# A list scheduler that counts changes between array tiles as TensorE time

## Chip, cores and metric

The kernel runs on one core of one Trainium2 chip. The metric is the device time of one execution in microseconds, from the first to the last instruction and what lies around them; lower is better. Times before and after are compared by the median of several runs.

## What is computed

A network of four layers on 512 positions with 1024 features, in fp32. The first block has a state-space layer and a latent-attention layer, each followed by a gated feed-forward layer; the second block has two layers that run three kinds of attention side by side. Cut to what matters:

```python
x = x + s5_mixer(rms_norm(x, mix_norm[0]), ...)            # layer 0: a state-space scan over 512 positions
x = x + swiglu_ffn(rms_norm(x, ffn_norm[0]), ...)
k, v = mla_shared_kv(rms_norm(x, kv_in_norm), ...)         # layer 1: latent attention, 16 heads
o = causal_block_attention(mla_queries(...), k, v)
x = x + o @ mla_w_o
x = x + swiglu_ffn(rms_norm(x, ffn_norm[1]), ...)
h = _layernorm(x, ...)                                      # second block
for layer in range(2):
    proj = h @ w_in[layer]                                  # three kinds of attention share it
    ya = _differential_attention(...) * silu(ag)            # 4 heads of 128, two softmaxes each
    yb = _forgetting_attention(...) * silu(bg)              # 4 heads of 64
    yc = _stick_breaking_attention(...) * silu(cg)          # 4 heads of 64
    h = _layernorm(ALPHA * h + concat(ya, yb, yc) @ w_out[layer], ...)
```

## The kernel before

Activations lie feature by feature: eight tiles of 128 features by 512 positions. A large product is made from three full-array products per 128x128 piece of the weights, since weights and activations are each split into a high and a low part of the fp32r type (`mm3`, line 651; names `wh_r`, `wl_r` for weights, `xh_r`, `xl_r` for activations). Weights come by DMA, ScalarE makes the high part, VectorE the low part.

Three stages use narrower tiles of TensorE's 128x128 array, named by rows*columns of the tile:

- The state-space scan (`s5_k`, `s5_x`, `s5_y`, `s5_o`, lines 995 to 1111): fp32 products on 128*32, 128*64 and 64*64 tiles. An fp32 product is two passes, two records in the trace.
- Latent attention (`attend`, line 1610): per head pair and block of 128 queries, two score products, softmax on VectorE and ScalarE, transposes of the probabilities (`nc.tensor.transpose`, one pass each, full array) and products with the values. Two heads share a PSUM bank; the values product of one head writes columns 0 to 63 of the array, that of the other columns 64 to 127 (`tile_position=(0, 64 * e)`). 32 such units; later `kv_part` and `q_part` products are mixed in.
- The second block's attentions (`attend_c`, `attend_a`, `attend_b`, `values`, from line 1777): the same shape of work, 32 units a layer; `values` (line 1897) is the one with 64-column tiles, the differential attention's product with the values uses the full array.

The order of all instructions is not written by hand. `Plan` (line 76) records every operation with its dependencies, then `schedule` (line 287) makes an order for all engines: twelve rounds of a forward list scheduling (`forward`, line 312) and a backward pass (line 370) that sets due times for the next round. The round with the earliest end by the planner's own costs is emitted. On TensorE, `forward` takes from the ready products the one with the earliest due time, plus a penalty where a weight load is longer than the product before it hides:

```python
i = min((i for i in ready[e] if at[i] <= t + 1e-9),
        key=lambda i: (due[i] + self.SWITCH * max(0.0, ops[i][6] - before), i))
t, before = max(t, free[e] + ops[i][6] - before), ops[i][1]
```

`ops[i][6]` is the load time of the product's weights, `before` the duration of the product ahead. The planner knows nothing of array tiles here. Where it foresees a gap on TensorE of more than 0.37 us and a PSUM bank is free, it puts idle-fill products (`fillers`, line 270, `ident` times `ident`) into it, so that the engine's clock stays up. Every recorded operation is issued from one helper, so the trace names L263 for nearly all; idle-fill products have L276. After the change the two lines are L265 and L278.

Of the kernel before, what the change touches and what calls it, by code (L numbers as in the profile page):

```python
# [20 lines left out]
P = 128  # L21
# [54 lines left out]
class Plan:  # L76
# [6 lines left out]
    SWITCH = 30.0  # L83
    TICK, DUTY = 10.24 / 3, 0.3735
    FILL, FLOOR = 0.22, 0.95
    parted = None
    EVERY_TABLE = (AF.Copy, AF.Identity, AF.Square)

# [25 lines left out]
    def switch(self, close, open):  # L114

        deps = {i: 0.0 for g in close for i in self.groups[g].used}
        for g in close:
            for i in self.groups[g].gate:
                deps[i] = 0.0
        i = len(self.ops)  # L120
        gone = [self.groups[g] for g in close]
        new = [Group(self, g) for g in open]

        def fn():
            for g in gone:
                g.exit()
            for g in new:
                g.enter(self.tc)

        self.ops.append((self.NONE, 0.0, 0.0, deps, self.clock, fn, 0.0, 0.0, None))  # L130
        for g in new:
            g.gate = [i]
            self.groups[g.name] = g
        return [Rings(g.make) for g in new]
# [77 lines left out]
    def add(self, eng, name, f, a, k, table=None):  # L212
        isap = lambda v: isinstance(v, (View, bass.AP))
        outs = [v for v in list(a[:1]) + [k.get("accum_out")] if isap(v)]
        ins = [v for v in list(a[1:]) + [v for x, v in k.items() if x != "accum_out"] if isap(v)]
        i, deps, order = len(self.ops), set(), set()
        if eng == self.ACT and name == "activation":
            func = a[2]
            if func not in self.EVERY_TABLE:
                table = "all" if self.table == "all" and func in (AF.Exp, AF.Ln) else func  # L220
        on_chip = lambda v: isinstance(v, View) or type(v.tensor).__name__ == "Tile"
        reads = [self.region(v) for v in ins if on_chip(v)]
        writes = [self.region(v) for v in outs if on_chip(v)]
        if table is not None:
            if table != self.table or name != "activation":
                self.table = table
                writes.append(("table", 0, 1, 0, 1))
            else:
                reads.append(("table", 0, 1, 0, 1))
        hit = lambda r, s: r[1] < s[2] and s[1] < r[2] and r[3] < s[4] and s[3] < r[4]  # L230
        inside = lambda r, s: r[1] >= s[1] and r[2] <= s[2] and r[3] >= s[3] and r[4] <= s[4]
        for r in reads:
            w, rd = self.mem.setdefault(r[0], ([], []))
            deps.update(o for s, o in w if hit(r, s))
        back = {}
        for r in writes:
            w, rd = self.mem.setdefault(r[0], ([], []))
            back[r] = {o for s, o in w + rd if hit(r, s)}
            deps.update(o for s, o in w if hit(r, s))
            deps.update(o for s, o in rd if hit(r, s) and self.ops[o][0] != eng)  # L240
            order.update(o for s, o in rd if hit(r, s) and self.ops[o][0] == eng)
        lag = {d: self.LAG[self.ops[d][0]][eng] for d in deps}
        lag.update((d, 0.0) for d in order if d not in deps)
        for g in {v.slot.group for v in ins + outs if isinstance(v, View)}:
            lag.update((d, 0.3) for d in g.gate)
            g.used.append(i)
        for r in reads:
            self.mem[r[0]][1].append((r, i))
        for r in writes:
            w, rd = self.mem[r[0]]  # L250
            w[:] = [x for x in w if not inside(x[0], r)] + [(r, i)]
            rd[:] = [x for x in rd if not inside(x[0], r) or x[1] == i]
        hold, done = self.cost(eng, name, a, k, outs[0] if outs else None, ins) if outs else (1.3, 1.3)
        real = lambda v: v.real() if isinstance(v, View) else v
        load, rows, idle = 0.0, 0.0, None
        if eng == self.PE:
            rows = a[1].shape[0] / P
            if name == "matmul" and k["start"] and self.filler is not None:
                idle = self.fillers(a[0], {o for r in writes for o in back[r]})

            load = a[1].shape[-1] / 1200.0 * (0.25 if a[1].dtype == BF16 else 1)
        self.ops.append((eng, hold, done, lag, self.clock,
                         lambda: f(*[real(v) for v in a], **{x: real(v) for x, v in k.items()}), load, rows, idle))  # L263
        if eng == self.PE:
            self.clock += hold + max(0.0, load - self.before)  # L265
            self.before = hold
        if self.urgent:
            self.first.add(i)
# [43 lines left out]
    def forward(self, due, succ):  # L312

        ops, N = self.ops, len(self.ops)
        left = [len(o[3]) for o in ops]
        free, at, ready, dma = [0.0] * 6, [0.0] * N, [[] for _ in range(6)], 0.0
        for i in range(N):
            if not left[i]:
                ready[ops[i][0]].append(i)
        order, end, before = [], [0.0] * N, 0.0  # L320


        self.fills, recent, work = {}, deque(), 0.0
# [5 lines left out]
        while len(order) < N:  # L329
            t, e = min((max(free[e], min(at[i] for i in ready[e])), e) for e in range(6) if ready[e])  # L330
            if e == self.PE:
                i = min((i for i in ready[e] if at[i] <= t + 1e-9),
                        key=lambda i: (due[i] + self.SWITCH * max(0.0, ops[i][6] - before), i))
                t, before = max(t, free[e] + ops[i][6] - before), ops[i][1]
                while recent and recent[0][0] < t - self.TICK:
                    work -= recent.popleft()[1]
                if t - free[e] > self.FILL + 0.15 and places:
                    j = min(places, key=places.get)
                    back = max(free[e], places[j])
                    n = min(int((t - back - 0.1) / self.FILL), math.ceil((self.FLOOR * self.TICK - work) / self.FILL))  # L340
                    if n > 0:
                        self.fills[i] = n, j
                        recent.append((t, n * self.FILL))
                        work += recent[-1][1]
                rate = 1.0 if work >= self.DUTY * self.TICK else 2.0
                recent.append((t, ops[i][1] * ops[i][7]))
                work += recent[-1][1]
                places.pop(i, None)
            else:
                i = min((i for i in ready[e] if at[i] <= t + 1e-9), key=lambda i: (due[i], i))  # L350
# [76 lines left out]
class View:  # L427
# [8 lines left out]
    def real(self):  # L436
        v = self.slot.tile
        for name, a, k in self.path:
            v = getattr(v, name)(*a, **k)
        return v  # L440
# [1802 lines left out]
```

## Time and profile before

| | us |
|---|---|
| median of 3 runs | 1882.0 (1877.3 to 1884.6) |
| profiled execution | 1880.2 |
| its span | 1878.5 |
| TensorE busy | 1822.5 |
| VectorE busy | 1158.0 |
| ScalarE busy | 838.9 |
| GpSimd busy | 546.5 |

Busy time is the union of an engine's records. Matmul records overlap: a product 512 columns wide is shown with 0.39 us, while the next one starts 0.23 us after it. So on TensorE the distance of starts tells a price, not the duration shown. The stages follow each other: scan to 337 us, first feed-forward layer to 628, latent attention and its projections to 939, second feed-forward layer and layer norm to 1304, the two layers of the second block to the end.

### The profile page before, as it was taken

To read this page: it belongs to the slowest core of one execution; us is meant where nothing else is said; L and a number is where in the kernel's file an instruction comes from. 1 tells how busy PE (TensorE), PEld (TensorE's weight loads), DVE (VectorE), ACT (ScalarE), POOL (GpSimd) and SP (SyncE) were. 2 spreads that over 40 slices of the span, in tenths; PEclk is the share of its full clock that TensorE was granted. 3 is DMA by queue.
4 is the path that set the end of the run, shared out by engine and by line. 5 is a ranking of instruction groups with operands and counts; after the bars stand their busy time and mean duration, and the time that the engine had idled before them with its cause. 6 is when DMAs were issued, how large, how long until landed. Compare 5 with 4: busy or idle time off the path is not lost.

```text
span 1878.5 us, 26997 instructions
## 1 busy us (share of the span) xinstructions
PE 1822.5 (97%) x10270; PEld 1464.9 (78%) x10270; DVE 1158.0 (62%) x2245; ACT 838.9 (45%) x1572; POOL 546.5 (29%) x650
## 2 busy tenths in 40 slices
PE   8899999999999999999999999999999999989997
PEld 5556888888888777678888888987778798778877
DVE  9995365344446677755434444664798763488875
ACT  4223243222223577643222222435767643566764
POOL 4892111001012185411101101630542071153205
PEclk8999999999999999999999999999999999999999
DMA  4533332323333220023332333432012132211113
GB/s 141 127 85 88 101 99 90 101 90 93 98 92 88 91 72 25 12 85 92 99 90 92 91 98 97 115 105 88 34 58 68 57 113 82 76 42 61 57 57 113
DMA packets 73137, 157.86 MB, mean 84 GB/s; under 512 B 26416, under 2 KB 34864, under 8 KB 73008
## 3 DMA queue, kind: packets, MB, share of 16 engines
q1 hardware_dynamic: 73008, 156.15, 27.2%
q8 instruction: 80, 1.31, 0.3%
q14 instruction: 49, 0.40, 0.1%
HBM read 150.81 MB, written 4.72 MB: 83 GB/s over the span
## 4 chain that ended last, share of the span: by engine, by line
PE 75%; DVE 8%; POOL 5%; ACT 4%; issue 2%; DMA 1%; SPq 0%; ACTq 0%; DVEq 0%; POOLq 0%
PE bank L263 75%; DVE bl L263 3%; DVE s L263 2%; POOL x L263 2%; POOL bl L263 1%; ACT bl L263 1%; POOL acc_r L263 1%; DVE wl_r L263 1%; ACT wh_r L263 1%; DVE x L263 1%; ACT xh_r L263 0%; ACT bh L263 0%; DVE sm_r L263 0%; DVE xl_r L263 0%; ACT xl_r L263 0%
## 5 line engine op out<-in xcount | busy, mean ns | idle before, releaser
L263 ACT ACTIVATE wh_r<-wr_r 128x1024 fp32r<-128x1024 f32 (+2 forms) x270 | 278.2, 1031 | 582.5 <-PE bank L263 531.7
L263 PE MATMUL bank<-xh_r,wl_r 128*128 128x512 f32 (+1 forms) x1312 | 503.7, 388 | 11.8 <-DVE wl_r L263 11.8
L263 PE MATMUL bank<-xl_r,wh_r 128*128 128x512 f32 (+1 forms) x1312 | 503.6, 387 | 0.7 <-DVE xl_r L263 0.5
L263 PE MATMUL bank<-xh_r,wh_r 128*128 128x512 f32 (+1 forms) x1312 | 500.9, 388 | 0.4 <-ACT s L263 0.4
L263 DVE TENSOR_TENSOR wl_r<-wr_r,wh_r 128x1024 fp32r<-128x1024 f32 (+2 forms) x270 | 374.8, 1389 | 152.1 <-ACT wh_r L263 148.0
L263 PEld LDWEIGHTS bank<-xh_r,wl_r 128*128 128x128 f32 x1312 | 248.5, 190 | 66.2 <-DVE wl_r L263 14.0
L263 PEld LDWEIGHTS bank<-xl_r,wh_r 128*128 128x128 f32 x1312 | 248.2, 190 | 53.1 <-issue 2.6
L263 PEld LDWEIGHTS bank<-xh_r,wh_r 128*128 128x128 f32 x1312 | 247.4, 189 | 53.3 <-issue 3.3
L263 POOL TENSOR_TENSOR ff<-ff,ff 128x512 f32<-128x512 f32 x44 | 62.6, 1422 | 590.2 <-DVE ff L263 574.9
L263 PE MATMUL bank<-ff,wh_r 128*128 128x512 f32 (+1 forms) x816 | 224.8, 363 | 0.2 <-ACT ff L263 0.2
L263 DVE TENSOR_TENSOR ff<-bank,ff 128x512 f32<-128x512 f32 x88 | 60.8, 691 | 224.4 <-PE bank L263 224.3
L263 PE MATMUL bank<-bh,wh_r 128*128 128x512 f32 (+1 forms) x656 | 179.9, 357 | 1.3 <-ACT bh L263 0.9
L263 PEld LDWEIGHTS bank<-ff,wh_r 128*128 128x128 f32 x816 | 145.4, 188 | 26.8 <-DVE ff L263 1.1
L263 PE MATMUL bank<-ff,wl_r 128*128 128x512 f32 (+1 forms) x408 | 146.4, 363 | 1.0 <-DVE wl_r L263 1.0
L263 DVE TENSOR_TENSOR x<-x,bank 128x256 f32<-128x256 f32 (+1 forms) x112 | 57.5, 530 | 131.4 <-PE bank L263 131.3
L263 PEld LDWEIGHTS bank<-bh,wh_r 128*128 128x128 f32 x656 | 114.4, 193 | 18.0 <-issue 2.4
L263 POOL TENSOR_TENSOR acc_r<-acc_r,sq_r 128x256 f32<-128x256 f32 (+1 forms) x63 | 75.0, 1191 | 162.8 <-ACT sq_r L263 162.7
L263 PE MATMUL bank<-bh,wl_r 128*128 128x512 f32 (+1 forms) x328 | 113.8, 356 | 0.0
L263 POOL TENSOR_TENSOR s<-s,s 128x256 f32<-128x256 f32 (+6 forms) x116 | 96.3, 858 | 34.9 <-DVE s L263 33.3
L263 ACT ACTIVATE ff<-ff 128x512 f32<-128x512 f32 x88 | 55.0, 626 | 74.3 <-POOL ff L263 68.8
L263 PEld LDWEIGHTS bank<-ff,wl_r 128*128 128x128 f32 x408 | 76.1, 188 | 14.0 <-DVE wl_r L263 1.2
L263 ACT ACTIVATE bl<-bank 128x256 f32<-128x256 f32 (+3 forms) x142 | 62.9, 453 | 52.9 <-PE bank L263 51.7
(258 smaller groups left out, 2822.6 us busy)
## 6 DMA issues: line engine op xcount, KB each, us to landing
wr_r<-w_gu SPq DMA_DIRECT2D x88, 512.0 KB, 3.5
wr_r<-w_in2f SPq DMA_DIRECT2D x48, 512.0 KB, 3.3
wr_r<-w_dn SPq DMA_DIRECT2D x37, 448.0 KB, 3.3
wr_r<-w_out SPq DMA_DIRECT2D x22, 512.0 KB, 3.3
wr_r<-w_dn SPq DMA_DIRECT2D x16, 512.0 KB, 3.5
wr_r<-w_in2v SPq DMA_DIRECT2D x16, 512.0 KB, 3.8
wr_r<-w_glu SPq DMA_DIRECT2D x12, 512.0 KB, 3.6
wr_r<-w_o SPq DMA_DIRECT2D x8, 512.0 KB, 3.2
```

Of the source, the lines that this page charges most:

```text
L263: lambda: f(*[real(v) for v in a], **{x: real(v) for x, v in k.items()}), load, rows, idle))
```

## The change

Each product gets a kind, `part`: 64 or 128 rows, and the number of 64-column groups in its tile, with a value of its own for transposes. In `forward`, a ready product of another kind than the last one is chosen only if it is due more than 3 us (`KEEP`) ahead of every ready one of the same kind, and a change of kind costs 0.15 us of TensorE's time in the plan (`TILES`). The recorded operations and their dependencies are the same. The function `switch` gets one more `None` in its tuple.

```diff
+    TILES, KEEP = 0.15, 3.0
...
-        load, rows, idle = 0.0, 0.0, None
+        load, rows, idle, part = 0.0, 0.0, None, None
         if eng == self.PE:
             rows = a[1].shape[0] / P
+            part = (64 if a[1].shape[0] <= 64 else P, P if name == "transpose" else a[1].shape[-1] // 64)
...
-                         lambda: f(*[real(v) for v in a], **{x: real(v) for x, v in k.items()}), load, rows, idle))
+                         lambda: f(*[real(v) for v in a], **{x: real(v) for x, v in k.items()}), load, rows, idle, part))
...
-        order, end, before = [], [0.0] * N, 0.0
+        order, end, before, part = [], [0.0] * N, 0.0, None
...
                 i = min((i for i in ready[e] if at[i] <= t + 1e-9),
-                        key=lambda i: (due[i] + self.SWITCH * max(0.0, ops[i][6] - before), i))
-                t, before = max(t, free[e] + ops[i][6] - before), ops[i][1]
+                        key=lambda i: (due[i] + self.SWITCH * max(0.0, ops[i][6] - before)
+                                       + self.KEEP * (ops[i][9] != part), i))
+                t, before = max(t, free[e] + ops[i][6] - before + self.TILES * (ops[i][9] != part)), ops[i][1]
+                part = ops[i][9]
```

First place: TensorE in latent attention, one softmax unit of two heads with four blocks of keys. `bank6_75` collects the products with the values (`mh_2` holds values, `ml_15` and `ml_16` the transposed probabilities of the two heads, by turns), `ident` marks transposes, the 128x384 and 128x512 rows are projections of later heads. It stood like this before:

```order
L263 MATMUL bank4_73<-ident_77,ml_7_4361 128x128 x2
L263 MATMUL bank1_70<-mh_4_2286,xh_r5_51_106 128x384
L263 MATMUL bank1_70<-mh_3_2285,xl_r5_53_107 128x384
L263 MATMUL bank6_75<-ml_16_4370,mh_2_2284 64x128
L263 MATMUL bank6_75<-ml_15_4369,mh_2_2284 64x128
L263 MATMUL bank6_75<-ml_16_4370,mh_2_2284 64x128
L263 MATMUL bank6_75<-ml_15_4369,mh_2_2284 64x128
L263 MATMUL bank6_75<-ml_16_4370,mh_2_2284 64x128
L263 MATMUL bank6_75<-ml_15_4369,mh_2_2284 64x128
L263 MATMUL bank5_74<-ident_77,ml_18_4372 128x128 x4
L263 MATMUL bank4_73<-ident_77,ml_17_4371 128x128 x4
L263 MATMUL bank6_75<-ml_16_4370,mh_2_2284 64x128
```

The same unit's products with the values stand like this now:

```order
L265 MATMUL bank1_70<-mh_3_2299,xh_r4_47_104 128x384
L265 MATMUL bank1_70<-mh_4_2300,xh_r4_47_104 128x384
L265 MATMUL bank6_75<-ml_15_4383,mh_2_2298 64x128
L265 MATMUL bank6_75<-ml_16_4384,mh_2_2298 64x128
L265 MATMUL bank6_75<-ml_15_4383,mh_2_2298 64x128
L265 MATMUL bank6_75<-ml_16_4384,mh_2_2298 64x128
L265 MATMUL bank6_75<-ml_15_4383,mh_2_2298 64x128
L265 MATMUL bank6_75<-ml_16_4384,mh_2_2298 64x128
L265 MATMUL bank6_75<-ml_15_4383,mh_2_2298 64x128
L265 MATMUL bank6_75<-ml_16_4384,mh_2_2298 64x128
L265 MATMUL bank4_73<-ident_77,ml_7_4375 128x128 x2
L265 MATMUL bank5_74<-ident_77,ml_18_4386 128x128 x4
```

The eight 64-column products of the unit now follow each other without a break; before, six stood together, one ahead of these rows and one behind two groups of transposes.

Second place: TensorE in the second block, first layer, the first products with the values (`bank7_76`, heads in `bl_17` and `bl_20`). Before the change:

```order
L263 MATMUL bank7_76<-bl_17_8862,bl_10_8855 64x128
L263 MATMUL bank1_70<-xl_r4_49_105,wh_r2_139_124 128x512
L263 MATMUL bank6_75<-ident_77,bl_18_8863 128x128
L263 MATMUL bank1_70<-xh_r4_47_104,wl_r2_141_125 128x512
L263 MATMUL bank1_70<-xh_r5_51_106,wh_r2_139_124 128x512
L263 MATMUL bank1_70<-xl_r5_53_107,wh_r2_139_124 128x512
L263 MATMUL bank1_70<-xh_r5_51_106,wl_r2_141_125 128x512
L263 MATMUL bank1_70<-xh_r6_55_108,wh_r2_139_124 128x512
L263 MATMUL bank7_76<-bl_20_8865,bl_10_8855 64x128
```

The same two products after the change:

```order
L265 MATMUL bank1_70<-xh_r0_31_96,wl_r2_141_125 128x512
L265 MATMUL bank7_76<-bl_17_8879,bl_10_8872 64x128
L265 MATMUL bank7_76<-bl_20_8882,bl_10_8872 64x128
L265 MATMUL bank5_74<-ident_77,bl_21_8883 128x128 x2
L265 MATMUL bank0_69<-xh_r3_43_102,wh_r0_125_118 128x512
L265 MATMUL bank0_69<-xl_r3_45_103,wh_r0_125_118 128x512
```

The two heads' products, eight rows apart before, now follow each other, with a group of transposes next to them.

Third place: TensorE early in the scan stage, idle-fill products (L276 before, L278 now). Before the change, the first of them:

```order
L263 MATMUL bank5_74<-xh_r7_59_110,wl_r2_141_125 128x512
L276 MATMUL bank4_73<-ident_77 32x128 x6
L263 MATMUL bank4_73<-s5_28_268,s5_60_300 32x128
L263 MATMUL bank6_75<-ident_77,s5_64_304 128x128 x4
L263 MATMUL bank4_73<-s5_28_268,s5_60_300 32x128 x7
```

After the change, where the first of them stand:

```order
L265 MATMUL bank6_75<-s5_29_269,s5_63_303 32x128 x8
L278 MATMUL bank3_72<-ident_77 128x128 x2
L265 MATMUL bank6_75<-s5_2_242,s5_66_306 64x128 x2
L278 MATMUL bank3_72<-ident_77 128x128 x2
L265 MATMUL bank4_73<-ident_77,s5_64_304 128x128 x4
L278 MATMUL bank3_72<-ident_77 128x128 x8
L265 MATMUL bank4_73<-s5_30_270,s5_60_300 32x128
L278 MATMUL bank3_72<-ident_77 128x128 x6
L265 MATMUL bank5_74<-ident_77,s5_64_304 128x128 x4
```

More idle-fill products stand between the scan's small products; over the whole order they go from 18 to 50.

## Rows read from the trace of the kernel before

**Rows 1.** The page, part 1: busy us (share of span) xinstructions of each engine.

```profile
PE 1822.5 (97%) x10270; PEld 1464.9 (78%) x10270; DVE 1158.0 (62%) x2245; ACT 838.9 (45%) x1572; POOL 546.5 (29%) x650
```

**Rows 2.** Windows: A:B length, busy us (xinstructions) per engine, TensorE clock, DMA share, GB/s.

```profile
83.00:147.00 64.00, 58.79 (x680) 38.72 (x679) 63.67 (x84) 21.05 (x41) 57.50 (x64) 1.00 0.39 101
660.00:820.00 160.00, 159.80 (x986) 116.23 (x986) 120.22 (x394) 113.56 (x300) 89.50 (x162) 1.00 0.13 39
1210.00:1240.00 30.00, 26.92 (x206) 25.99 (x206) 25.89 (x55) 15.04 (x28) 24.61 (x24) 0.94 0.34 113
```

**Rows 3.** Chain that ended last, shares by line, in 660:820, 1304:1525 and 1640:1840.

```profile
by line: PE bank L263 94.3%; ACT ml L263 1.7%; DVE ml L263 1.3%; ACT mh L263 0.9%; ACT wh_r L263 0.6%; DVE yq_r L263 0.5%; DVE nw_r L263 0.4%; ACT ir_r L263 0.2%; issue 0.2%; DVE ir_r L263 0.1%
...
by line: PE bank L263 60.0%; DVE bl L263 14.0%; issue 6.2%; POOL bl L263 4.1%; ACT bl L263 3.4%; ACT bh L263 2.6%; POOL bh L263 2.5%; DVE wl_r L263 2.5%; DVE bh L263 2.1%; DVE sm_r L263 1.0%; DVE xl_r L263 0.5%; ACT wh_r L263 0.4%; ACT xh_r
...
by line: PE bank L263 47.6%; DVE bl L263 14.4%; POOL bl L263 7.8%; ACT bl L263 7.6%; ACT xh_r L263 3.8%; issue 3.7%; ACT xl_r L263 3.0%; DVE wl_r L263 1.8%; DVE xh_r L263 1.8%; DVE sm_r L263 1.7%; ACT wh_r L263 1.5%; DVE xl_r L263 1.4%; POO
```

**Rows 4.** TensorE's timeline from 1320 us: start us, duration us, engine, operation, count.

```profile
1320.09 0.40 PE L263 MATMUL bank<-xh_r,wh_r 128*128 128x512 f32 x1
1320.42 0.43 PE L263 MATMUL bank<-bl,bl 128*64 128x128 f32 x2
1320.78 0.50 PE L263 MATMUL bank<-xl_r,wh_r 128*128 128x512 f32 x1
1321.12 0.39 PE L263 MATMUL bank<-xh_r,wl_r 128*128 128x512 f32 x1
1321.35 0.39 PE L263 MATMUL bank<-xh_r,wh_r 128*128 128x512 f32 x1
...
1322.05 0.40 PE L263 MATMUL bank<-xh_r,wh_r 128*128 128x512 f32 x1
1322.38 0.44 PE L263 MATMUL bank<-bl,bl 128*64 128x128 f32 x4
1322.75 0.73 PE L263 MATMUL bank<-bh,bh 128*128 128x512 f32 x2
```

**Rows 5.** TensorE's timeline, second half of latent attention.

```profile
809.61 0.40 PE L263 MATMUL bank<-xh_r,wh_r 128*128 128x512 f32 x1
809.94 0.88 PE L263 MATMUL bank<-ml,mh 128*64 128x128 f32 x12
...
811.08 0.39 PE L263 MATMUL bank<-xh_r,wl_r 128*128 128x512 f32 x1
```

**Rows 6.** TensorE's timeline, scan stage, one transpose.

```profile
41.10 0.39 PE L263 MATMUL bank<-xl_r,wh_r 128*128 128x512 f32 x1
41.33 0.27 PE L263 MATMUL bank<-ident,s 128*128 128x128 f32 x1
...
41.68 0.39 PE L263 MATMUL bank<-xh_r,wh_r 128*128 128x512 f32 x1
```

**Rows 7.** TensorE's timeline, second block, seven transposes.

```profile
1370.11 0.41 PE L263 MATMUL bank<-xh_r,wh_r 128*128 128x512 f32 x1
1370.35 0.93 PE L263 MATMUL bank<-ident,bl 128*128 128x128 f32 x7
...
1371.35 0.39 PE L263 MATMUL bank<-xh_r,wl_r 128*128 128x512 f32 x1
```

**Rows 8.** Groups by shape, 0:147, then 147:337: xcount | busy us, mean ns.

```profile
L263 PE MATMUL bank<-s,s 64*64 64x128 f32 x166 | 16.1, 284 | 2.1 <-POOL s L263 2.1
...
L263 PE MATMUL bank<-s,s 64*64 64x128 f32 x90 | 8.3, 283 | 0.0
```

**Rows 9.** TensorE's timeline, second block, eight passes of fp32 products.

```profile
1421.31 0.39 PE L263 MATMUL bank<-xh_r,wl_r 128*128 128x512 f32 x1
1421.54 1.05 PE L263 MATMUL bank<-bl,bl 128*128 128x128 f32 x8
...
1422.67 0.39 PE L263 MATMUL bank<-xh_r,wh_r 128*128 128x512 f32 x1
```

**Rows 10.** TensorE's waits, 1304 to 1878.5 us: total us, times, longest.

```profile
PE bank L263 <- POOL bl L263: 7.8, 10, 1.7
```

More of the change, by code (lines that the diff above doesn't have):

```diff
@@ L128, in fn @@
                 g.enter(self.tc)
-        self.ops.append((self.NONE, 0.0, 0.0, deps, self.clock, fn, 0.0, 0.0, None))
+        self.ops.append((self.NONE, 0.0, 0.0, deps, self.clock, fn, 0.0, 0.0, None, None))
         for g in new:
```

## The prediction

> **What bounds the kernel now.** The page's busy times come first: TensorE is busy in 97% of the span, the next engine, VectorE, in 62% [rows 1]. Its matmuls overlap their neighbours in the records, so whether that 97% is a limit has to be read stage by stage, from the windows [rows 2] and the chain that ended last [rows 3]. Three stretches answer differently.
>
> - State-space scan, 83 to 147 us: VectorE is busy 63.67 of 64 us, TensorE has gaps. VectorE bounds.
> - Latent attention, 660 to 820 us: TensorE is busy 159.80 of 160 us, and 94.3% of the chain is TensorE. TensorE bounds.
> - The two attention stretches of the second block, 1304 to 1525 and 1640 to 1840 us: TensorE holds 60.0% and 47.6% of the chain; the rest is VectorE, GpSimd and ScalarE, waited for in turn.
>
> Time taken off TensorE is thus worth its full size in the second, about half in the third, nearly nothing in the first.
>
> **What a change between tiles costs on TensorE.** Starts of neighbouring matmuls give the price. A full-array product 512 columns wide starts 0.23 us after the one before (1321.12 to 1321.35 in [rows 4]). One 64-column product (two passes) between two such products makes it 1321.12 - 1320.09 = 1.03 us from the full-array product ahead of it to the second one behind it. Without it that would be 2 x 0.23 = 0.46, so this visit costs 0.57 us. Two of them at both column positions cost no more: 0.70 us to the next start (1322.05 to 1322.75) against 0.69 for one (1320.09 to 1320.78). Six products (12 passes, three pairs) cost 811.08 - 809.61 - 0.46 = 1.01 us [rows 5]. So two further pairs took 0.44: **0.22 us a pair** (or a lone product), and 0.57 - 0.22 = **0.35 us for the visit itself**, in and out.
>
> The scheduler also counts a transpose as a tile of its own kind. The trace gives that no price: one transpose among full-array products costs 41.68 - 41.10 - 0.46 = 0.12 us [rows 6], seven in a row 1371.35 - 1370.11 - 0.46 = 0.78, which is 0.11 each [rows 7]. Bringing transposes together saves nothing, though their groups fall from 236 to 144.
>
> [...]
>
> **The change, part by part.** No product is added or dropped but the idle-fill ones; only the order moves, and all counts here are taken over TensorE's whole order before and after.
>
> 1. *Visits.* Stretches on tiles narrower than the full array fall from 167 to 113: scan 40 to 23, latent attention 56 to 40, second block 68 to 48, one elsewhere. Times 0.35 us: 6.0, 5.6, 7.0 and 0.35 us.
> 2. *Lone products.* A 64-column product that stood apart from its partner wasted the second column position. Lone visits fall from 22 to 7 in latent attention and from 31 to 14 in the second block; pairs or lone products to be paid fall from 98 to 89 and from 103 to 94. 9 x 0.22 = 2.0 us in each.
> 3. *What of it is on the path.* Latent attention: 7.6 x 0.943 = 7.1 us. Second block: 9.0 x 0.54 (between 0.476 and 0.600) = 4.9 us. Scan: of the 256 passes on the 64x64 tile 90 run after 147 us, when VectorE is done with its load [rows 8], so a third of 6.0 counts: 2.0 us. For the rest of the scan nothing: VectorE's 63.67 of 64 us covers it. The one visit elsewhere I leave out. **Sum 14.0 us.** All of it on the path would be 23 us, the one end.
> 4. *Idle-fill products.* These keep TensorE active in gaps that the scheduler foresees; they rise from 18 to 50. Eight passes (four products of that size) cost 1422.67 - 1421.31 - 0.46 = 0.90 us [rows 9], so 0.22 a product and 32 x 0.22 = 7.0 us if no gap were there. They lie where nothing was ready, so I take 0, hidden by the wait; the cover goes if the foreseen gap does not come.
> 5. *Transposes held together and products held back.* KEEP lets a product of the same kind pass one of another kind due up to 3 us earlier. Where TensorE bounds, order alone costs nothing; where softmax is waited for, it can. TensorE's waits on GpSimd in the second block were 7.8 us in 10 waits, 0.78 each [rows 10]; nothing in the trace shows how many more there will be. Taken as 0 net; the upper end is the second rival.
> 6. *Other engines and queues.* SyncE, GpSimd, ScalarE and VectorE get no new instruction. Their orders shift by a few places with TensorE's, since one planner makes all of them; no DMA is added, and the DMA engines stand at 0.39 and 0.13 of their time in the first two stretches of [rows 2], so weights do not become the bound.
>
> The profiled execution took 1880.2 us, 1.8 below the median of 1882.0. 1880.2 - 14.0 = **1866 us**, against that median about 0.8% less.
>
> **Rivals.** A measurement of this kernel can tell about 0.5%, 9.4 us, from no change.
>
> *The time becomes waiting: 1880 us.* Products of one kind end sooner, and TensorE then waits for softmax. For it: in the second block other engines hold half of the chain [rows 3], and the scheduler itself now foresees more gaps, 50 idle-fill products instead of 18. Against it: in latent attention TensorE had no gap, so at least those 7 us should come.
>
> *A wait takes the place of the visits: 1891 us, slower.* The place is the second block's attention, 64 softmax units in two layers. If a score product or a transpose is passed by products of the kept kind while VectorE or GpSimd runs dry, that unit's chain ends later. If half of the units got one more wait of 0.78 us [rows 10], that is 25 us: 1880.2 - 14.0 + 25 = 1891. It decides above 0.22 us a unit (14.0 / 64), and makes the kernel measurably slower from 0.37 us a unit ((14.0 + 9.4) / 64). Against it: the scheduler tries twelve orders and keeps the shortest by its own costs, which hold these chains.
>
> *The clock falls: 1901 us.* The granted clock is not always full: 1.00 in latent attention, but 0.94 at 1210 to 1240 us, where TensorE was idle for 3 of 30 us [rows 2]. If longer groups of transposes brought 0.94 to the three attention stretches (160 + 221 + 200 = 581 us), 6% of them, 35 us, would be lost: 1880.2 - 14.0 + 35 = 1901. Against it stand the 1.00 in a stage with hundreds of transposes, and that the longest group stays at twelve of them, 12 x 0.11 = 1.3 us.
>
> **How the numbers follow.** Forecast 0.66, time becomes waiting 0.22, new wait 0.09, clock 0.03. The forecast's own range is 1857 (all 23 us realised) to 1873 (the 7.1 us of latent attention alone); about one in ten of it lies within 0.5% of no change. So faster by over 0.5%: 0.60; within 0.5%: 0.06 + 0.22 = 0.28; slower: 0.09 + 0.03 = 0.12. The range for 8 in 10 goes from 1854, a little under all 23 us since fewer visits may also shorten a few waits, to 1884, which takes in the case of time lost to waiting and half of what idle-fill products can cost, and leaves out the last two rivals.
>
> **What would show it.** In the profile after: the 64-column products of latent attention in rows of 8 or more passes, that stage some 7 us shorter with TensorE still busy throughout; the scan until 147 us no shorter, with more idle time on TensorE; the second block 3 to 6 us shorter with slightly longer waits. Wrong it would be if a visit's price were not 0.35 us in the new order, if latent attention kept its length with gaps on TensorE, or if waits for VectorE, GpSimd or ScalarE in the second block grew by more than 5 us.

## The result and the profile after

The change makes the kernel slower: 1892.11 us (median of 7 runs, 1889.99 to 1894.02) against 1882.01 us, a ratio of 1.0053 with a 95% interval of 1.0044 to 1.0062. The prediction was 1866 us, faster by 0.8%, with a range up to 1884. It was wrong in sign, and the time fell outside the range. The profiled execution of the change spans 1890.4 us, 11.9 more than that of before.

First the busy time of the engines on the page of the changed kernel (busy us, share of the span, instructions):

```profile
PE 1819.1 (96%) x10334; PEld 1479.0 (78%) x10334; DVE 1151.1 (61%) x2245; ACT 840.5 (44%) x1572; POOL 540.1 (29%) x650
```

TensorE has 64 instructions more than in [rows 1], the two passes of each of the 32 additional idle-fill products, and is busy 3.4 us less in a span that is 11.9 us longer: its idle time (span less busy time) grows from 56.0 to 71.3 us. The windows of the changed kernel say where (columns as in [rows 2]):

```profile
83.00:150.00 67.00, 54.89 (x652) 38.29 (x651) 61.64 (x82) 18.93 (x37) 61.58 (x76) 0.91 0.35 90
660.00:820.00 160.00, 155.58 (x1001) 115.22 (x1000) 122.20 (x408) 115.78 (x312) 91.16 (x165) 1.00 0.12 39
...
1310.00:1530.00 220.00, 207.32 (x1302) 173.37 (x1301) 172.04 (x389) 145.37 (x319) 72.41 (x86) 0.99 0.20 64
1650.00:1850.00 200.00, 188.37 (x1184) 156.58 (x1183) 157.13 (x365) 133.28 (x289) 62.73 (x71) 0.99 0.17 57
```

In latent attention, where TensorE had 0.2 us of idle time [rows 2], it now has 4.4. The chain that ended last, in 660 to 820 us of the changed kernel, answers to the first line of [rows 3]:

```profile
by line: PE bank L265 63.6%; DVE ml L265 10.1%; ACT ml L265 8.6%; POOL ml L265 3.1%; ACT mh L265 3.1%; issue 2.3%; POOL yk_r L265 2.1%; POOL yq_r L265 1.6%; DVE mh L265 1.0%; DVE yq_r L265 0.8%; DVE wl_r L265 0.8%; ACT xh_r L265 0.7%; ACT w
```

TensorE's share of it fell from 94.3% to 63.6%: the chain now runs in part through the softmax on VectorE and ScalarE (the `ml` tiles). For the lengths of the stages the GpSimd product of the gate in the two feed-forward stages serves as a mark (the tile `ff`, asked for from 290 to 840 and from 840 to 1300 us: name, count, shortest/median/longest in ns, first and last start in us). Of before:

```profile
L263 POOL TENSOR_TENSOR ff<-ff,ff x19: 1285/1291/2012, 293.6 to 577.1; 128x512 f32<-128x512 f32 x19
L263 POOL TENSOR_TENSOR ff<-ff,ff x22: 1286/1291/2007, 861.5 to 1180.0; 128x512 f32<-128x512 f32 x22
```

Of the change:

```profile
L265 POOL TENSOR_TENSOR ff<-ff,ff x19: 1290/1291/2015, 299.5 to 583.0; 128x512 f32<-128x512 f32 x19
L265 POOL TENSOR_TENSOR ff<-ff,ff x22: 1287/1291/2007, 865.6 to 1184.2; 128x512 f32<-128x512 f32 x22
```

Up to the last mark of the first feed-forward stage the change is 5.9 us later (577.1 to 583.0), where the scan is the stage whose visits fall (40 to 23). All 5.9 are there at the first of these marks already (293.6 to 299.5), so they arise ahead of it. From the last mark of the first feed-forward stage to the first mark of the second, with latent attention in between, it gains 1.8 (284.4 to 282.6) where 7.1 was forecast. From the last mark (1180.0 and 1184.2) to the end of the span, with the second block's attention, it loses 7.7 (698.5 to 706.2), where 4.9 less was forecast. The feed-forward stage itself keeps its length (318.5, 318.6).

How a wait looks: TensorE's timeline in latent attention of the changed kernel (start us, duration us, engine, operation, count; in brackets the idle time before it and who ended it):

```profile
665.74 0.52 PE L265 MATMUL bank<-mh,xh_r 128*128 128x384 f32 x2
666.10 0.34 PE L265 MATMUL bank<-mh,xl_r 128*128 128x384 f32 x1
667.25 0.44 PE L265 MATMUL bank<-ident,ml 128*128 128x128 f32 x2 [0.81 <-POOL ml L265]
667.44 0.60 PE L265 MATMUL bank<-mh,xh_r 128*128 128x384 f32 x2
667.87 0.34 PE L265 MATMUL bank<-mh,xl_r 128*128 128x384 f32 x1
668.06 0.51 PE L265 MATMUL bank<-mh,xh_r 128*128 128x384 f32 x2
```

And what it waits for, in the timeline of all engines:

```profile
665.67 1.52 POOL L265 TENSOR_TENSOR ml<-ml,yk_r 128x256 f32<-128x256 f32 x1
```

GpSimd is done at 667.19, and the two transposes start at 667.25. The 384-column products that the planner put behind them start after them and show no wait of their own. Whether their inputs were there before 667.25 us these rows don't tell; if they were, the planner put the two transposes in front of ready work, and the 0.81 us are the price.

### The profile page after: what moved, and what is told of

Read it like the earlier page. It is cut to its first block, busy times and chain, and to the rows that moved or that the text cites. A ratio compares the mean times of both kernels' runs of the same rounds, so it can differ in the third digit from the quotient of the medians.

```text
span 1890.4 us, 27124 instructions
## 1 busy us (share of the span) xinstructions
PE 1819.1 (96%) x10334; PEld 1479.0 (78%) x10334; DVE 1151.1 (61%) x2245; ACT 840.5 (44%) x1572; POOL 540.1 (29%) x650
## 3 DMA queue, kind: packets, MB, share of 16 engines
q1 hardware_dynamic: 73008, 156.15, 26.8%
## 4 chain that ended last, share of the span: by engine, by line
PE 70%; DVE 11%; ACT 6%; POOL 5%; issue 2%; ACTq 0%; POOLq 0%; DVEq 0%
PE bank L265 70%; DVE bl L265 5%; ACT bl L265 2%; DVE wl_r L265 2%; DVE s L265 1%; POOL x L265 1%; POOL s L265 1%; ACT bh L265 1%; POOL bl L265 1%; DVE ml L265 1%; POOL acc_r L265 1%; ACT ml L265 1%; DVE bh L265 1%; DVE x L265 1%; ACT xh_r L265 1%
## 5 line engine op out<-in xcount | busy, mean ns | idle before, releaser
L265 DVE TENSOR_TENSOR wl_r<-wr_r,wh_r 128x1024 fp32r<-128x1024 f32 (+2 forms) x270 | 370.6, 1374 | 146.9 <-ACT wh_r L265 142.7
L265 PE MATMUL bank<-bh,wh_r 128*128 128x512 f32 (+1 forms) x656 | 175.4, 354 | 1.5 <-ACT bh L265 0.6
L265 POOL TENSOR_TENSOR s<-s,s 128x512 f32<-128x512 f32 (+6 forms) x116 | 98.1, 877 | 44.5 <-DVE s L265 43.7
```

## The experiments

All were timed in five rounds, beside the kernel before on the same chip (medians 1879.9 to 1882.2). Unless another base is named, the edit is to the changed kernel. A *visit* is a stretch on tiles narrower than the full array, as in the prediction. The counts are of each kernel's TensorE order.

**One half at a time.** The change has two numbers: TILES charges 0.15 us of planned time at each change of kind, KEEP lets a product of the same kind pass one that is due up to 3 us earlier.

```diff
-    TILES, KEEP = 0.15, 3.0
+    TILES, KEEP = 0.15, 0.0
```

> The change with KEEP = 0: a change of kind still costs 0.15 us in the plan, but no due product is passed any more. TensorE's order then has 144 visits to narrow tiles (167 before, 113 with the change), 223 groups of transposes (236, 144) and 8 idle-fill products (18, 50). Theory held-back (KEEP lets kept-kind products pass due ones, softmax ends later and TensorE waits): the waits of the change go, the 23 visits saved at 0.35 us stay in part, so 1874 to 1880 us, against 1882 before. Rival false charge (the 0.15 us charged for transposes makes the plan wrong): still slower than before, 1885 to 1892. Rival any new order (a reshuffle of a tuned order costs about this much by itself): 1885 to 1895.

Measured: 1913.89 us, ratio 1.0172 (1.0158 to 1.0186); 144 visits. The time lies above the ranges of all three theories. The charge alone is worse than the whole change, by 22 us. So the hold cannot be the only cause, and in the change it even takes some of the charge's damage back.

```diff
-    TILES, KEEP = 0.15, 3.0
+    TILES, KEEP = 0.0, 3.0
```

> The change with TILES = 0: products of one kind are still kept together for up to 3 us of due time, but the plan charges nothing for a change. 131 visits, 175 groups of transposes, 63 idle-fill products. Theory held-back: as slow as the change or slower, 1888 to 1898 us, with TensorE's waits on ScalarE, VectorE and GpSimd in latent attention, where there were almost none before. Rival false charge: the harm goes with the charge, 1872 to 1882. Rival any new order: 1885 to 1895.

Measured: 1893.6 us, ratio 1.0061 (1.0049 to 1.0073); 131 visits, 63 idle-fill products. The hold alone is as slow as the change.

**Transposes counted as what TensorE's trace showed them to be**, not a tile of their own (0.12 us alone, 0.11 each in seven [rows 6, 7]). Narrow tiles keep their kinds, with the charge and the hold unchanged:

```diff
-            part = (64 if a[1].shape[0] <= 64 else P, P if name == "transpose" else a[1].shape[-1] // 64)
+            part = (64 if a[1].shape[0] <= 64 else P, 2 if name == "transpose" else a[1].shape[-1] // 64)
```

> The change, but a transpose gets the kind of a full-array product, so only narrow tiles count as another kind; KEEP = 3 and TILES = 0.15 stay. 88 visits (167 before, 113 with the change), 1 lone visit, 222 groups of transposes (236, 144), 25 idle-fill products (18, 50). Theory held-back in its narrow form (what hurts is that transposes, which softmax results wait for, are held back against products and products against transposes, for nothing): the waits of the change go and 79 visits at 0.35 us are saved, half of it on the path: 1862 to 1874 us. Held-back in its wide form (keeping any kind for 3 us hurts, narrow tiles too): 1882 to 1895. Rival any new order: 1885 to 1895.

Measured: 1868.88 us, ratio 0.9932 (0.992 to 0.9944); 88 visits. Whether transposes are a kind decides the sign: with them 0.5% slower, without them 0.7% faster. Its marks:

```profile
L265 POOL TENSOR_TENSOR ff<-ff,ff x19: 1282/1289/2011, 292.8 to 576.3; 128x512 f32<-128x512 f32 x19
L265 POOL TENSOR_TENSOR ff<-ff,ff x22: 1286/1288/2006, 852.5 to 1171.0; 128x512 f32<-128x512 f32 x22
```

Against before the first part is 0.8 us shorter, the part with latent attention 8.2 shorter (852.5 - 576.3 = 276.2 against 284.4), and the end 5.5 shorter (1864.0 - 1171.0 = 693.0 against 698.5). The forecast had 2.0, 7.1 and 4.9 there, and 1866 us in all, but for 54 visits fewer. Here 79 are saved, for which the forecast's 14.0 us, scaled by the visits, would be some 20 (an estimate). So some two thirds of the saving came, and that the time is only 2.9 us from 1866 is in part luck.

**Idle-fill.** In the change without the idle-fill products (this leaves out those products, whose results nobody uses):

```diff
-                if t - free[e] > self.FILL + 0.15 and places:
+                if False:
```

> The change without idle-fill products (the condition that puts them in is never true): 50 fewer of them, 110 visits, 143 groups of transposes. Theory held-back: idle-fill stands in waits, so nothing changes but the clock in a few places: 1888 to 1896 us. Rival idle-fill (32 more idle-fill products at 0.22 us are what the change costs): 1882 to 1886 us, about 7 to 10 us below the change.

Measured: 1888.18 us, ratio 1.0031 (1.0019 to 1.0043). The 50 products cost 3.9 us of the 10.1. Much of them is in the scan, as the group by line and shape of 0 to 150 us in the changed kernel shows (40 passes, two a product; before there were 12):

```profile
L278 PE MATMUL bank<-ident 128*128 128x128 f32 x40 | 6.8, 322 | 0.7 <-DVE s L265 0.7
```

**Charge and hold on narrow tiles alone.** The edit of the third experiment, with KEEP = 0.0 and then with TILES = 0.0:

```diff
-    TILES, KEEP = 0.15, 3.0
+    TILES, KEEP = 0.15, 0.0
```

> Transposes counted as full-array products, TILES = 0.15, KEEP = 0: the plan charges for narrow tiles alone, which the trace prices at 0.35 us a visit, and passes no due product. 140 visits, 216 groups of transposes. Theory false time (a charge for transposes that the chip does not take lets the plan's TensorE run late, so the plan puts products first whose inputs the chip does not have yet): the charge is close to the truth here, so the 32 us that the charge alone cost go: 1868 to 1884 us. Rival any charge (moving TensorE's time in the plan at all does the harm): 1900 to 1915. Rival any new order: 1885 to 1900.

Measured: 1883.59 us, ratio 1.0012 (1.0003 to 1.0021); 140 visits. They are 27 fewer than before, 9.5 us on TensorE at 0.35, and none of it shows in the time.

```diff
-    TILES, KEEP = 0.15, 3.0
+    TILES, KEEP = 0.0, 3.0
```

> Transposes counted as full-array products, TILES = 0, KEEP = 3: only narrow tiles are kept together, and no time is charged. 98 visits, 4 lone visits, 219 groups of transposes. Theory transposes held (with KEEP alone at 1893.6 us, what hurt was that transposes and products were held back against each other for nothing): 1864 to 1876 us. Rival wide holding (keeping narrow tiles hurts as well, and the charge is needed to repair it): 1884 to 1896.

Measured: 1871.19 us, ratio 0.9943 (0.993 to 0.9956); 98 visits. On narrow tiles the charge alone does next to nothing in either direction, and the hold alone brings nearly all of the gain. What the charge cost in the first experiment (1913.9 against 1883.6 here) is thus the transposes' charge: 30 us.

**The charge on transposes alone**, narrow tiles not told apart:

```diff
-            part = (64 if a[1].shape[0] <= 64 else P, P if name == "transpose" else a[1].shape[-1] // 64)
+            part = name == "transpose"
...
-    TILES, KEEP = 0.15, 3.0
+    TILES, KEEP = 0.15, 0.0
```

> The kind is only whether a product is a transpose, TILES = 0.15, KEEP = 0: nothing but the false charge is left, some 219 groups in and out, 2 x 219 x 0.15 = 66 us over the plan. 151 visits, 219 groups of transposes. Theory false time: most of the 32 us of the charge alone: 1898 to 1916 us. Rival narrow charge (the harm of the charge alone came with narrow tiles): 1878 to 1888. Rival any new order: 1885 to 1900.

Measured: 1905.77 us, ratio 1.0124 (1.0107 to 1.0141). It costs 24 us by itself, with 16 visits fewer than before.

**Is it that the plan's TensorE is too slow?** In the kernel before, with no kinds at all, every product's planned time on TensorE made 4.5% longer, then 4.5% shorter:

```diff
-            return (t + 0.003,) * 2
+            return (t * 1.045 + 0.003,) * 2
```

> The kernel before, with each product's time in the plan 4.5% longer and no kinds at all: about the same 66 us too much over the plan, but spread over all products. 153 visits (167 before). Theory false time, if any lateness of the plan's TensorE does it: 1895 to 1915 us. If it has to fall at the transposes themselves, where softmax is waited for: 1878 to 1890. Rival any new order: 1885 to 1900.

Measured: 1892.42 us, ratio 1.0056 (1.0043 to 1.0069). That is slower, but by less than the theory's range; it lies in that of the rival of any new order. On its page TensorE is busy 1821.1 us of a span of 1890.7, so the work is nearly that of before (1822.5), and the idle time grows from 56.0 to 69.6: the loss is waiting.

```diff
-            return (t + 0.003,) * 2
+            return (t * 0.955 + 0.003,) * 2
```

> The counterpart of the slow plan: the kernel before with each product's time in the plan 4.5% shorter, no kinds. 165 visits. Theory false time in its one-sided form (a plan whose TensorE is late puts products first whose inputs are not there yet; one that is early only puts them back): 1872 to 1885 us, no slower than before. Two-sided form (any wrong time in the plan costs as much): 1889 to 1900. Rival any new order: 1885 to 1900.

Measured: 1874.16 us, ratio 0.9966 (0.9953 to 0.9978). The slower plan costs 11 us and the faster one gains 6 to 8, with 153 and 165 visits (before 167). That speaks for the theory's one-sided form. Each is a single order, and steps of this size are not far from what two orders can differ by (the longer hold below), so it is support and not proof.

**Control: does any other order move the time?** In the kernel before:

```diff
-    SWITCH = 30.0
+    SWITCH = 29.0
```

> A control: the kernel before with SWITCH 29 in place of 30, which has no meaning for tiles or times but gives another order (165 visits, 233 groups of transposes, 21 idle-fill products). If any new order of this planner moves the time by some 10 us, the verdicts of single variants mean little: beyond 1872 or 1892. If not: 1877 to 1887 us.

Measured: 1881.52 us, ratio 1.0002 (0.9993 to 1.0011). This order moves nothing. It is close to the old one (233 groups of transposes against 236), so it does not bound what a more different order can do.

**A longer hold.** The edit of the third experiment, with the charge near the trace's price (0.35 us a visit, so 0.175 each way) and the hold doubled:

```diff
-    TILES, KEEP = 0.15, 3.0
+    TILES, KEEP = 0.175, 6.0
```

> Transposes as full-array products, TILES = 0.175 (half of the 0.35 us that the trace gives a visit) and KEEP = 6: 89 visits, 3 lone. An attempt at a better version. Theory transposes held and false time: narrow tiles alone may be held longer, as fast as the version with 3 us or a little faster, 1860 to 1871 us. Rival longest hold (6 us puts values products late): 1874 to 1884.

Measured: 1878.82 us, ratio 0.9984 (0.9975 to 0.9993); 89 visits. No visit fewer than with 3.0 and 0.15, and 9.9 us slower: the longer hold finds nothing more to bring together. The charge was raised too, so how much of the 9.9 is the hold's is not divided by this run. It also shows that two orders with the same number of visits can differ by some 10 us. The steps of 22 to 30 us, which telling transposes apart costs, are clear of that.

**The third experiment without idle-fill** (the edits of the third and the fourth together):

```diff
-                if t - free[e] > self.FILL + 0.15 and places:
+                if False:
```

> Transposes as full-array products, TILES = 0.15, KEEP = 3, and no idle-fill products: 86 visits, 25 idle-fill products fewer than with them. The change lost some 4 us of its 10 to them (1888.2 without, 1892.1 with). If idle-fill costs 0.1 us a product here too: 1864 to 1868 us. If the clock falls more without them: 1869 to 1876.

Measured: 1865.29 us, ratio 0.9914 (0.9899 to 0.993). At most a little faster than with it: the intervals overlap.

**The two effects on transposes apart**, narrow tiles as in the third experiment in both. `part` holds two kinds, one for the hold and one for the charge; first the charge alone tells transposes apart:

```diff
+            rows_ = 64 if a[1].shape[0] <= 64 else P
-            part = (64 if a[1].shape[0] <= 64 else P, P if name == "transpose" else a[1].shape[-1] // 64)
+            part = ((rows_, 2 if name == "transpose" else a[1].shape[-1] // 64),
+                    (rows_, P if name == "transpose" else a[1].shape[-1] // 64))
...
-                                       + self.KEEP * (ops[i][9] != part), i))
-                t, before = max(t, free[e] + ops[i][6] - before + self.TILES * (ops[i][9] != part)), ops[i][1]
+                                       + self.KEEP * (ops[i][9][0] != part[0]), i))
+                t, before = max(t, free[e] + ops[i][6] - before + self.TILES * (ops[i][9][1] != part[1])), ops[i][1]
```

> The change with the hold (KEEP) on narrow tiles alone and the charge (TILES) on transposes as well: 86 visits, 196 groups of transposes, 39 idle-fill products. Theory false time (in the change the charge on transposes is what costs the 23 us against 1868.9): 1885 to 1897 us. Theory transposes held (the hold costs it): 1866 to 1873.

Measured: 1897.69 us, ratio 1.0091 (1.0074 to 1.0107); 86 visits, 0.7 us above the first range and far from the second. Then the hold alone tells them apart (the two indices 0 and 1 exchanged in the last two lines):

```diff
+                                       + self.KEEP * (ops[i][9][1] != part[1]), i))
+                t, before = max(t, free[e] + ops[i][6] - before + self.TILES * (ops[i][9][0] != part[0])), ops[i][1]
```

> The change with the charge on narrow tiles alone and the hold on transposes as well: 125 visits, 30 lone, 166 groups of transposes, 48 idle-fill products. Theory false time: 1868 to 1876 us. Theory transposes held: 1886 to 1896, near the 1893.6 of the hold without any charge.

Measured: 1895.69 us, ratio 1.0081 (1.0065 to 1.0098); 125 visits. Either effect alone undoes more than the whole gain. With both it is 1892.1: they do not add, and each costs nothing where the other is already there.

**The best version:** the third experiment, without idle-fill, on a plan that is 4.5% faster:

```diff
-            return (t + 0.003,) * 2
+            return (t * 0.955 + 0.003,) * 2
```

> Transposes as full-array products, TILES = 0.15, KEEP = 3, no idle-fill, and each product's time in the plan 4.5% shorter: 88 visits, no lone one. If an early plan helps here as it did without kinds (7.7 us): 1856 to 1861 us. If the right kinds already gave what it gives: 1862 to 1869.

Measured: 1859.02 us, ratio 0.9884 (0.9866 to 0.9901), faster than both kernels. Its chain in 660 to 820 us is TensorE's again, to 85.3%:

```profile
by line: PE bank L265 85.3%; POOL yq_r L265 4.3%; DVE ml L265 3.2%; ACT ml L265 1.4%; POOL ml L265 1.2%; DVE yq_r L265 0.9%; issue 0.8%; POOL yk_r L265 0.8%; DVE wl_r L265 0.8%; ACT wh_r L265 0.6%; ACT mh L265 0.2%; DVE yk_r L265 0.2%; DVE 
```

The pages of the last three versions that the next table compares (no kind for transposes, charge only, hold only):

```profile
PE 1794.1 (96%) x10284; PEld 1464.6 (79%) x10284; DVE 1146.2 (61%) x2245; ACT 838.5 (45%) x1572; POOL 543.2 (29%) x650
...
PE 1810.7 (96%) x10312; PEld 1471.9 (78%) x10312; DVE 1155.1 (61%) x2245; ACT 840.2 (44%) x1572; POOL 540.9 (29%) x650
...
PE 1819.5 (96%) x10330; PEld 1475.0 (78%) x10330; DVE 1156.5 (61%) x2245; ACT 838.4 (44%) x1572; POOL 546.7 (29%) x650
```

Side by side (visits, groups of transposes and idle-fill products in the order; TensorE's busy time and the rest of the span, in one profiled execution each; median time):

| kernel | transposes charged | transposes held | visits | groups | idle-fill | busy | idle | us |
|---|---|---|---|---|---|---|---|---|
| before | no | no | 167 | 236 | 18 | 1822.5 | 56.0 | 1882.0 |
| the change | yes | yes | 113 | 144 | 50 | 1819.1 | 71.3 | 1892.1 |
| no kind for transposes | no | no | 88 | 222 | 25 | 1794.1 | 69.9 | 1868.9 |
| charge only on them | yes | no | 86 | 196 | 39 | 1810.7 | 85.2 | 1897.7 |
| hold only on them | no | yes | 125 | 166 | 48 | 1819.5 | 74.3 | 1895.7 |

Without a kind for transposes TensorE is busy 28.4 us less than before and idle 13.9 more. The change is idle for nearly as long as that version (1.4 us more), and busy 25.0 us longer.

## Why the prediction was wrong

**Right: the price of a visit** (steps 1 and 2). In the changed kernel a visit of twelve passes in latent attention reads, on TensorE's timeline:

```profile
812.16 0.40 PE L265 MATMUL bank<-xh_r,wl_r 128*128 128x512 f32 x1
812.49 0.88 PE L265 MATMUL bank<-ml,mh 128*64 128x128 f32 x12
813.30 0.50 PE L265 MATMUL bank<-xh_r,wh_r 128*128 128x512 f32 x1
813.64 0.39 PE L265 MATMUL bank<-xl_r,wh_r 128*128 128x512 f32 x1
```

From the product ahead of it to the second one behind it 1.48 us pass; less 0.46 that is 1.02, against 1.01 in [rows 5]. With the transposes left in the full array, a saving came in the parts of the program that the prediction named, and TensorE's busy time fell by 28.4 us with 79 visits fewer.

**Failed: "Transposes held together and products held back ... Taken as 0 net" (step 5).** This is the step that decided the sign. It saw correctly that "Bringing transposes together saves nothing", and stopped there. A rule of order that saves nothing is not free: telling transposes apart makes 1868.9 into 1892.1 us, 23 us, and with the hold alone 1871.2 into 1893.6.

*The charge.* At 0.15 us a change, on a plan in which groups of transposes come and go some 144 to 236 times, it adds time to TensorE that the chip does not take (a transpose alone costs 0.12 us and each of seven 0.11 [rows 6, 7], so no price of that size shows). With the visits equal (86 and 88), the charge on transposes makes 1868.9 into 1897.7 us: 28.8 us that cannot be visits; at the prediction's 0.22 us the 14 additional idle-fill products are 3 of them. On the pages, whose spans differ by 31.9 us, 15.3 are idle time and 16.6 busy time. Of the 16.6 the idle-fill products are the 3; the rest is not accounted for. TensorE's waits for softmax tiles over the whole span show some of the idle time. Without the transposes' kind:

```profile
PE bank L265 <- ACT bl L265: 7.9, 8, 2.4
PE bank L265 <- POOL bl L265: 7.1, 7, 2.9
PE bank L265 <- DVE bl L265: 4.7, 9, 1.3
```

With the charge on transposes alone added:

```profile
PE bank L267 <- DVE bl L267: 15.3, 13, 3.5
PE bank L267 <- ACT bl L267: 10.4, 6, 4.1
```

There the row for GpSimd is gone, so the three rise from 19.7 to 25.7 us. The likely way, which the slow and the fast plan support: a planner whose TensorE runs late believes that softmax results will be there when TensorE comes to them. On the chip TensorE comes earlier, and waits, as it did for 0.81 us ahead of 667.25 us in the change. That the misplaced products are the cause one by one was not tried; that a slower planned TensorE alone costs 11 us, without any kinds, was, and that is less than half of the charge's 24 to 30.

*The hold.* With transposes as a kind that is kept, groups of transposes grow (222 to 166), and narrow products are kept apart by them: 125 visits instead of 88. At 0.35 us that is 13 us, and 23 more idle-fill products at 0.22 are 5: 18 of the 26.8 us between those two runs. The pages agree with the kind of loss: TensorE is busy 25.4 us longer and idle 4.4 longer. What makes the rest of the busy time is open. Here the cause is mostly that the change works against its own aim.

In the change both are present. Of the 23 us that steps 1 and 2 counted on TensorE, idle-fill at full price takes back 7; the span of the profiled execution rose by 11.9. So some 28 us were lost elsewhere: 15.3 as idle time, and some 13 as busy time, since that fell by 3.4 and not by 16. For those 13 a lower clock is a candidate (see the rivals). The waits that the trace lists for softmax tiles in the second block are, for the change:

```profile
PE bank L265 <- POOL bl L265: 8.9, 8, 2.4
...
PE bank L265 <- ACT bl L265: 5.3, 9, 1.4
PE bank L265 <- DVE bl L265: 4.8, 7, 1.1
```

Together 19.0 us, where before it was 11.3 (7.8 for GpSimd [rows 10], 1.8 and 1.7). But the version without the transposes' kind has 19.7 in the same rows and nearly the same idle time in all, and is 23 us faster because TensorE is busy 25.0 us less. Of these the 25 visits fewer are 9 (at 0.35) and the 25 idle-fill products fewer 5.5 (at 0.22); the rest is not divided. So these waits alone do not rank two orders: against before the change loses by waiting, against this version by work.

**Failed: "Latent attention: 7.6 x 0.943" (step 3).** The 94.3% was right for the old order and no property of the stage. The new order turned it into 63.6%, and 1.8 us came of the 7.1. Without a kind for transposes, and with more visits saved, the gain of that stage was 8.2 with 73.5% TensorE on the chain. The share of the chain says what a little less work is worth in the order that was traced; a rule that rewrites the order has to be asked first what it does to the share.

**Off in size: idle-fill products, "I take 0, hidden by the wait" (step 4).** Taking them out gives back 3.9 us of the change; the upper end of the step, 0.22 us each, would have been 11 for 50. The reason for 0, "They lie where nothing was ready", did not hold for all of them; the step had named the case of a foreseen gap that does not come, and no run shows how often it occurred.

**Scan (2.0 us, steps 3 and 6).** The saving did not come: the part up to the end of the first feed-forward stage became 5.9 us longer. Step 6 let the orders of the other engines "shift by a few places". In 83 to 150 us GpSimd's products on the scan's tiles hold 35.1% of the chain in the change, against 6.4% before, and VectorE is busy 61.64 of 67 us where it had next to no gap before [rows 2]. TensorE waits for the scan's end, here 4.02 us:

```profile
149.62 1.97 PE L265 MATMUL bank<-ident,s 64*64 64x64 f32 x32 [4.02 <-ACT s L265]
```

TensorE's granted clock falls around this wait: 1.00 from 145 to 147 us, 0.82 to 149, 0.50 from there to 158.5, then 1.00 to 162; before, it is 1.00 in all of these. These are the windows at the end of the scan, before and with the change (columns as in [rows 2]):

```profile
147.00:158.00 11.00, 10.52 (x148) 7.40 (x148) 6.50 (x10) 2.11 (x4) 3.25 (x5) 1.00 0.33 89
...
148.00:159.00 11.00, 8.86 (x94) 6.28 (x96) 4.38 (x6) 4.33 (x8) 3.48 (x3) 0.53 0.33 93
```

At 0.50 the 32 passes that start at 149.62 us take 1.90 us to the next start (151.52); before, at 1.00, 32 passes of the same form took 1.08 (153.73 to 154.81). From 153.4 us on the chain is TensorE's, and from there to 158.5 us the low clock costs some 2.2 us (an estimate from these two: 5.1 us less 5.1 x 1.08/1.90). So of the 5.9 us a part is the clock's, and the rest goes with the scan's later end. In the version without the transposes' kind the clock from 83 to 150 us is as low (0.92, against 0.91), but 1.00 from 146 to 157 us, and the part is 0.8 us shorter than before. What moved GpSimd's work onto the path was not tried.

**The rivals.** "A wait takes the place of the visits: 1891 us" has the time, with a chance of 0.09, and half of the mechanism: products that pass due ones make new waits. It had the place too narrow (the scan and latent attention lose as well) and missed the charge, which does as much damage without the hold. Its counterargument, that the planner keeps the shortest of twelve orders "by its own costs, which hold these chains", was the weak link: the charge on transposes put a wrong number into those costs. "The clock falls" named the attention stretches, and there nothing fell: 1.00 in latent attention and 0.99 in the second block, as before. But over the whole execution the mean granted clock is 0.983 in the runs of the change and 0.988 in those of before; in the profiled execution most of the difference lies in the scan. Over 54 executions of the kernel before, time goes with it: the 11 with a clock up to 0.986 span 1881.8 us on average, the 7 with 0.990 and more 1878.0. By that slope some 4 of the change's 10 us could be the clock's (an estimate from a correlation; no experiment set the clock). It is not needed for a loss: the hold alone is 12 us slower than before at 0.987, and the slower plan 11 us at 0.989. "The time becomes waiting: 1880 us" named the direction and stopped at zero.

**What the signs said.** Of the three that were to show it wrong, "latent attention kept its length with gaps on TensorE" came true but for 1.8 us. The waits for softmax tiles in the second block grew by 7.7 us, over the 5 that were named. The first sign, a visit's price other than 0.35 us, did not appear.

## What to carry to other kernels

A list scheduler's cost is a claim on the hardware: charge a change of kind only where neighbouring starts in the trace show its price. Here a charge that the trace does not show cost 24 to 30 us in three pairs of orders, with more waiting on TensorE (for softmax tiles, `bl`, 24.2 us against 12.7, 23.1 against 11.3 and 25.7 against 19.7). Before a rule of order is costed at nothing because it saves nothing, price its side: what it lets pass, what it splits, and what it does to the times in the plan. Then take the loss apart on the page, into busy and idle time of the engine that bounds: the two ask for different remedies. And the test is cheap: make the plan of the bounding engine a few per cent slower and faster, and see which way the time goes (here 1892.4 and 1874.2 us around 1882.0).

## What the runs showed that was not expected

- A plan with TensorE's times 4.5% shorter did better than the old one: 0.34% on the kernel before, and some 0.3% on the version without transposes' kind and idle-fill (1865.3 to 1859.0 us, in intervals that just touch at 0.990). That the planner's times were too long for TensorE all along is a likely reason, and not shown.
- The two effects on transposes do not add: 28.8 and 26.8 us alone, 23.2 together. By the pages the hold costs TensorE's busy time (25.4 of it), the charge both (16.6 busy, 15.3 idle).
- Keeping TensorE active with idle-fill did not pay in these orders. The granted clock from 83 to 150 us fell without it only from 0.91 to 0.90 in the change, and from 0.92 to 0.90 in the version without the transposes' kind. The change gained 3.9 us; the other version 3.6 (1868.9 to 1865.3), where the two intervals overlap and the spans of the profiled executions are equal, 1864.0 us, so that gain is not settled.
